# Two running sums per chunk for the convolution's taps, eight taps moved to GpSimd, two more gated pairs in three passes, the memory queries' copies ahead

## The chip, the cores and the metric

The kernel runs on one core of a Trainium2 chip. A core has five engines that each work through their own queue in order: TensorE (PE in the profile, with its weight loads as PEld), VectorE (DVE), ScalarE (ACT), GpSimd (POOL) and SyncE (SP), which here issues the loads of the weights. The metric is the device time of one execution in microseconds (us); lower is better. Before the change it is 976.33 us, the median of three runs (974.7 to 977.23).

## The reference

The kernel computes a decoder trunk of two layers on 256 tokens of width 1024 in fp32. Layer 0 is a SwiGLU feed-forward half step, then a mixer, then a second feed-forward half step; layer 1 has the same shape with another mixer. The change lies in the mixer of layer 0. Cut to that:

```python
u = hn @ a_w_in                                   # 1024 -> 768 + 768 + 256
a, gate = split(u[..., :1536], 2)                 # the gated pair
h = a * sigmoid(gate)
h = depthwise_conv(h, dw_kernel, 31 taps, causal) + dw_bias
primary = silu(layer_norm(h, ln_g, ln_b))         # mean and variance over the 768 channels
q_mem = u[..., 1536:]                             # 4 heads of 64, attention over 256 memory rows
mem_out = memory_attention(rms_norm(q_mem), ...)
h_out = x + concat(primary, mem_out) @ w_o
```

The convolution is per channel: for each of the 768 channels, 31 products of a shifted row of 256 tokens with one number are summed, and the bias is added.

## The kernel before

Activations lie transposed: 128 channels on the partitions, the 256 tokens along the free dimension. The 768 convolution channels are six chunks of 128 (c = 0 to 5). Weights come in chunks of 1 MB ([128, 2048], two halves of 1024 columns); one chunk holds the two halves of one gated pair, that is the 128 columns of `a` and of `gate` for one c. Three raw buffers hold loaded chunks.

**Three passes or whole.** TensorE multiplies either *in three passes* or *whole*. For three passes a half chunk is split by `half_chunk`: ACT makes the high part `wh` (`hi`, L184), DVE subtracts it from the raw weights to get the low part `wl` (`lo`, L188), and TensorE runs high x high, high x low and low x high (`mm3`); four `wh` and four `wl` buffers rotate. Whole, TensorE takes raw fp32 weights and activations (`whole_group`), and no other engine works on the weights. In `glu_in` the chunks c < `SPLIT_CHUNKS` (2) go in three passes and the others whole.

**Gating.** `glu_out` (high priority for the planner) scales the sums by the row norm (`cgs`, `cas` on DVE), takes the sigmoid on ACT (`cs`), and DVE writes the product into `hp` (L833; four smaller products, L838, for chunk 5). `hp` is the front of one large SBUF tile `hc`; the rest of `hc` holds `whole`, the convolution's results `cv` and the second layer's memory rows `my1`.

**Convolution.** `conv(c)` shares the 31 taps of a chunk between two engines, by `DVE_TAPS` = (14, 31, 0, 31, 18) and `POOL_TAPS` = (17, 0, 31, 0, 13) for chunks 0 to 4. DVE's share is one chain: the first tap writes a sum in PSUM (L857), each further tap is one `scalar_tensor_tensor` (L861), sum = window x tap + sum, reading the window in SBUF and the sum in PSUM. GpSimd's share: ACT writes the first tap with the bias into `cv` (L849), then for each further tap ACT scales the window into a buffer `cq` (L852; two buffers), and GpSimd adds it to `cv` (L853). Where both have a share, DVE adds its sum to `cv` at the end (L864). Chunk 5 is done on TensorE with diagonal matrices (`cvp`, L151). ACT also does eight scalings for `my1` (L876).

**What follows on TensorE**, in a fixed order: the memory queries' projection `mq`; the diagonal matmuls for chunk 5 (`cvp`); six steps of the second layer's memory keys and values (`mkv`); the transposes of the memory queries (`mq0p`, L154), which ACT copies out as `q0T` (L459, in `to_heads_T`); two more `mkv` steps; the scores of two pairs of memory heads (`am00s`, `am01s`), which need `q0T`; two `mkv` steps; and `lnm`, the mean over the channels, which takes the six chunks of `cv` in the order 5, 0, 1, 2, 3, 4. Between `mq` and `mq0p` lie ACT's squares (L434), DVE's sums and products (L436, L519, L521), GpSimd's power (L523) and DVE's last product (L526).

**Order.** From the convolution's start TensorE's instructions keep program order (`state["order"]`). The other engines' order is set by a planner when the kernel is built: it takes instructions as they get ready by its own estimate, those emitted earlier first, and those in `high_priority` before all. On the chip each queue then runs in that order. `behind(i, other)` makes instruction i come after `other` in the queue. Attention's steps later are in order by hand (`in_order`).

Of the kernel before, what the change touches and what calls it, by code (L numbers as in the profile page):

```python
# [9 lines left out]
F32 = mybir.dt.float32  # L10
# [3 lines left out]
AF = mybir.ActivationFunctionType  # L14
ALU = mybir.AluOpType
AX = mybir.AxisListType

P = 128
DM = 1024
KD = DM // P  # L20
SEQ = 256
NT = SEQ // P
DFF = 2816
KF = DFF // P
# [6 lines left out]
CC = PW // P  # L31
TAPS = 31
PAD = TAPS - 1
# [6 lines left out]
NB = 2 * MW  # L40
WARM = 12
MASKED = 1e30
SPLIT_CHUNKS = 2

DVE_TAPS = (14, 31, 0, 31, 18)
POOL_TAPS = (17, 0, 31, 0, 13)

HALF_CH = P // 2
SHIFTS = (TAPS + 1) // 2
# [1 line left out]
MEM_AT = 9  # L51
FIRST_CAT = 3
TURN_AT = 2
SLACK = 64
HOMES = {"ahs": 64, "bhs": 64, "chs": 64, "dhs": 64, "my0": 192, "by0": 192, "ay0": 128, "cat0": 128, "cat1": 128}
Q_AT = 6
# [29 lines left out]
def tile_kernel(ctx: ExitStack, tc: tile.TileContext, w, xT, memT, pos, vec, hg, const, out):  # L86
    nc = tc.nc
# [3 lines left out]
    tp = ctx.enter_context(tc.tile_pool(name="tp", bufs=2))  # L91
    op = ctx.enter_context(tc.tile_pool(name="op", bufs=4))
# [23 lines left out]
    q = HC // 2  # L116
# [14 lines left out]
    state = {"flip": False, "chunk": 0, "half": 0, "raw": None, "order": "", "last": {}}  # L131

    def behind(i, other):
        tc.add_manual_dep(i.ins, other.ins.name,
                          mybir.DependencyInfo(mybir.DependencyClass.NoSync, mybir.DependencyReason.DATA),
                          reason="issue order")
# [16 lines left out]
    def transp(*a, **k):  # L153
        in_order("P", nc.tensor.transpose(*a, **k))  # L154
# [44 lines left out]
    def tiles_of(n_half):  # L199
        for n in range(n_half):  # L200
            wh, wl = half_chunk()
            for i in range(8):
                yield wh[:, i * P:(i + 1) * P], wl[:, i * P:(i + 1) * P]
# [46 lines left out]
    def psum(name, tag="mm", bufs=4):  # L250
        return ps.tile([P, 512], F32, name=name, tag=tag, bufs=bufs)


    def at_home(t, name):
        a = HOMES.get(name, 0) // 4
        return t[:, a:a + t.shape[1] - SLACK].rearrange("p (k a s) -> p k a s", a=2, s=SEQ)

    def y_tiles(name):
        return at_home(yp.tile([P, KD * 2 * SEQ + SLACK], F32R, name=name, tag="y"), name)

    def y_both(name):
        whole = at_home(yp.tile([P, KD * 2 * SEQ + SLACK], F32, name=name + "w", tag="y"), name)
        return y_tiles(name), whole[:, :, 0]
# [67 lines left out]
    def ffn(name, y, acc, nexts, store=False, both=False, hook=None, after=None, hook_down=None, rb=None):  # L331

        hs = at_home(hp_.tile([P, KF * 2 * SEQ + SLACK], F32R, name=name + "hs", tag="hs"), name + "hs")
        first = acc is None
# [96 lines left out]
    def heads_norm(name, t, n):  # L431

        sq = tp.tile([P, MW], F32, name=name + "q", tag="sq")
        nc.scalar.activation(sq[:, :n * HD], t, AF.Square)  # L434
        ms = tp.tile([P, 4], F32, name=name + "m", tag="ms")
        nc.vector.tensor_reduce(ms[:, :n], sq[:, :n * HD].rearrange("p (h d) -> p h d", d=HD), axis=AX.X, op=ALU.add)  # L436
        return ms

    def rope(name, q3, t):

        n = q3.shape[1]
        a = tp.tile([P, 4, ROT], F32, name=name + "a", tag="ra")
        b = tp.tile([P, 4, ROT], F32, name=name + "b", tag="rbb")
        nc.vector.tensor_tensor(a[:, :n], q3[:, :, :ROT], cosT[:, t, None, :].to_broadcast([P, n, ROT]), op=ALU.mult)
        nc.vector.tensor_tensor(b[:, :n, :HALF], q3[:, :, HALF:ROT],
                                sinT[:, t, None, :HALF].to_broadcast([P, n, HALF]), op=ALU.mult)
        nc.vector.tensor_tensor(b[:, :n, HALF:], q3[:, :, :HALF],
                                sinT[:, t, None, HALF:].to_broadcast([P, n, HALF]), op=ALU.mult)
        nc.vector.tensor_tensor(q3[:, :, :ROT], a[:, :n], b[:, :n], op=ALU.add)

    def gain_b(g, n):
        return gt[:, None, g * HD:(g + 1) * HD].to_broadcast([P, n, HD])

    def to_heads_T(name, src, dst, pair0, t, tag="aux"):

        pp = psum(name, tag, 2)
        for i in range(2):
            transp(pp[:, i * P:(i + 1) * P], src[:, i * P:(i + 1) * P], ident)
        nc.scalar.activation(dst[:, pair0:pair0 + 2, t * P:(t + 1) * P],  # L459
                             pp[:, :2 * P].rearrange("p (a b) -> p a b", a=2), AF.Copy)  # L460

    def proj(name, y, *uses):

# [48 lines left out]
    def queries(name, e, g, dst, pair0, rot, scaler, defer=None):  # L512


        def use(t, o):
            ms = heads_norm(f"{name}s{t}", o, 4)
            qg = tp.tile([P, MW], F32, name=f"{name}t{t}", tag="tok")
            q3 = qg.rearrange("p (h d) -> p h d", d=HD)
            nc.vector.tensor_tensor(q3, o.rearrange("p (h d) -> p h d", d=HD), gain_b(g, 4), op=ALU.mult)  # L519
            v = tp.tile([P, 4], F32, name=f"{name}v{t}", tag="hv")  # L520
            nc.vector.tensor_scalar(v, ms, e[:, t:t + 1], None, op0=ALU.add)  # L521
            c = tp.tile([P, 4], F32, name=f"{name}c{t}", tag="hr")
            nc.gpsimd.tensor_tensor(c, v, mhalf[:, :4], op=ALU.pow)  # L523
            if rot:
                rope(f"{name}o{t}", q3, t)
            scaler.tensor_tensor(q3, q3, c[:, :, None].to_broadcast([P, 4, HD]), op=ALU.mult)  # L526
            def turn():
                to_heads_T(f"{name}p{t}", qg, dst, pair0, t, "aux" if defer is None else "sc")
            if defer is None:
                turn()  # L530
            else:
                defer.append(turn)
        return use
# [87 lines left out]
    def go(head, n):  # L621
        for _ in range(n):
            next(head)
# [148 lines left out]

    hc = hp_.tile([P, KF * 2 * SEQ + SLACK], F32, name="hc", tag="hs")
    hp = hc[:, :CC * (PAD + SEQ)].rearrange("p (c s) -> p c s", c=CC)
    whole = hc[:, CC * (PAD + SEQ):CC * (PAD + SEQ) + 2 * SEQ].rearrange("p (i s) -> p i s", i=2)
    cv = hc[:, KF * SEQ:KF * SEQ + CC * SEQ].rearrange("p (c s) -> p c s", c=CC)
    my1 = hc[:, (KF + CC) * SEQ:(KF + CC + KD) * SEQ].rearrange("p (k s) -> p k s", k=KD)
    nc.gpsimd.memset(hp[:, :, :PAD], 0.0)
    acc_p = [psum("cvp0", "aux", 2), psum("cvp1", "sc", 2)]

# [2 lines left out]
    tap = [[vt[:, V_TAP + c * TAPS + i:V_TAP + c * TAPS + i + 1] for i in range(TAPS)] for c in range(CC)]  # L783
    bias = [vt[:, V_CB + c:V_CB + c + 1] for c in range(CC)]
    rr = {}

    def whole_group(o, raw, i, ks):
        for k in ks:
            mmul(o[:, :SEQ], raw[:, (i * KD + k) * P:(i * KD + k + 1) * P], y[1][:, k], start=k == 0, stop=k == KD - 1)

    def glu_in(c):

        pa, pg = psum(f"ca{c}"), psum(f"cg{c}")
        if c == 0:
# [16 lines left out]
            return  # L811
        elif c < SPLIT_CHUNKS:
            for k, wt in enumerate(tiles_of(1)):
# [28 lines left out]
    def win(c, i):  # L842
        return hp[:, c, i:i + SEQ]

    def conv(c):
        nd, np_ = DVE_TAPS[c], POOL_TAPS[c]
        bi = bias[c]
        if np_:
            nc.scalar.activation(cv[:, c], win(c, nd), AF.Identity, scale=tap[c][nd], bias=bias[c])  # L849
            for i in range(nd + 1, nd + np_):  # L850
                q = tp.tile([P, SEQ], F32, name=f"cq{c}_{i}", tag="cvq")
                nc.scalar.activation(q, win(c, i), AF.Copy, scale=tap[c][i])  # L852
                state["pool"] = nc.gpsimd.tensor_tensor(cv[:, c], cv[:, c], q, op=ALU.add)  # L853
            bi = None
        if nd:
            o = acc_p[c == 1][:, (c == 3) * SEQ:((c == 3) + 1) * SEQ]
            nc.vector.tensor_scalar(o, win(c, 0), tap[c][0], bi, op0=ALU.mult,  # L857
                                    op1=ALU.bypass if bi is None else ALU.add)
            for i in range(1, nd):
                end = i == nd - 1 and bi is not None  # L860
                nc.vector.scalar_tensor_tensor(cv[:, c] if end else o, win(c, i), tap[c][i], o,  # L861
                                               op0=ALU.mult, op1=ALU.add)
            if bi is None:
                state["last"]["V"] = nc.vector.tensor_tensor(cv[:, c], o, cv[:, c], op=ALU.add)  # L864

    qT = cp.tile([P, 2, SEQ], F32, name="q0T", tag="q0T")
    kT, v = kv0
    for c in range(CC):
# [5 lines left out]
        if 0 < c < CC - 1:  # L874
            for k in range(2 * c - 2, 2 * c):
                behind(nc.scalar.activation(my1[:, k], mT[:, k], AF.Copy,  # L876
                                            scale=vt[:, V_MEM + KD + k:V_MEM + KD + k + 1]), state["func"])
# [5 lines left out]
    last = psum("cvp2")  # L883
# [3 lines left out]
    for g in range(2):  # L887
        for p in range(2):
            r = slice(p * HALF_CH, (p + 1) * HALF_CH)
            dst = cv[g * HALF_CH:(g + 1) * HALF_CH, CC - 1].rearrange("p (t q) -> p q t", q=2)[:, p]  # L890
# [17 lines left out]

    go(mem1, 6)
    for turn in turns:  # L910
        turn()
    go(mem1, 2)
    go(pairs[0], 1)
    go(pairs[1], 1)
# [87 lines left out]
    for k, (wh, wl, *_) in enumerate(halves):  # L1002
        for m in range(KD):
            s = slice(m * P, (m + 1) * P)
# [41 lines left out]
    n = len(pairs)  # L1046
    for p in range(n + 1):
        if p < n:
            go(pairs[p], 1)
        if p == TURN_AT:  # L1050
            for turn in turns:
# [142 lines left out]
```

## Time and profile before

| what | value |
|---|---|
| median of three runs | 976.33 us (974.7 to 977.23) |
| profiled execution, its own time | 976.35 us |
| its span, first to last instruction | 974.6 us |
| TensorE busy | 962.7 us, 99% of the span |
| VectorE busy | 743.9 us, 76% |
| ScalarE busy | 599.7 us, 62% |
| GpSimd busy | 123.6 us, 13% |
| granted TensorE clock | 1.00 |
| gated pairs, convolution, memory queries | about 204 to 270 us of the span |

Busy time is the sum of an engine's instructions. Rows of a timeline show the start, the length, the engine, the line, the operation and what it writes and reads; "xN" joins N neighbours of one kind. Instructions of DVE overlap a little at their edges, so that starts are nearer than lengths say. Rows of a line's own view show how many there are, the shortest, median and longest length in ns, and the first and last start.

### The profile page before, as it was taken

To read this page: it belongs to the slowest core of one execution; us is meant where nothing else is said; L and a number is where in the kernel's file an instruction comes from. 1 tells how busy PE (TensorE), PEld (TensorE's weight loads), DVE (VectorE), ACT (ScalarE), POOL (GpSimd) and SP (SyncE) were. 2 spreads that over 40 slices of the span, in tenths; PEclk is the share of its full clock that TensorE was granted. 3 is DMA by queue.
4 is the path that set the end of the run, shared out by engine and by line. 5 is a ranking of instruction groups with operands and counts; after the bars stand their busy time and mean duration, and the time that the engine had idled before them with its cause. 6 is when DMAs were issued, how large, how long until landed. Compare 5 with 4: busy or idle time off the path is not lost.

```text
span 974.6 us, 15375 instructions
## 1 busy us (share of the span) xinstructions
PE 962.7 (99%) x5784; PEld 840.1 (86%) x5784; DVE 743.9 (76%) x1328; ACT 599.7 (62%) x1154; POOL 123.6 (13%) x143
## 2 busy tenths in 40 slices
PE   8999999999999999999999999999998999999998
PEld 6888888898779888888888888888995898888887
DVE  7988776779977888777776877777789588888663
ACT  6676577857676665655556665565557656565542
POOL 0011000128713000000122000000152030000000
PEclk9999999999999999999999999999999999999999
DMA  8655555533325554555554555556442055555560
GB/s 312 241 199 179 197 189 188 202 130 131 114 102 188 204 213 174 203 186 176 203 183 174 183 206 178 207 177 212 177 174 87 27 194 213 180 210 174 190 219 23
DMA packets 26427, 173.47 MB, mean 178 GB/s; under 512 B 3184, under 2 KB 4848, under 8 KB 6000
## 3 DMA queue, kind: packets, MB, share of 16 engines
q1 hardware_dynamic: 26064, 172.31, 50.3%
q8 instruction: 45, 0.74, 0.3%
q14 instruction: 30, 0.25, 0.1%
q10 hardware_dynamic: 288, 0.17, 0.1%
HBM read 171.43 MB, written 1.05 MB: 177 GB/s over the span
## 4 chain that ended last, share of the span: by engine, by line
PE 92%; ACT 2%; DVE 2%; POOL 2%; DMA 1%; issue 1%; POOLq 0%; ACTq 0%; DVEq 0%
PE cg L151 7%; PE do L151 6%; PE bo L151 6%; PE dg L151 6%; PE bg L151 6%; PE bu L151 6%; PE co L151 6%; PE cu L151 6%; PE ao L151 6%; PE du L151 6%; PE ag L151 6%; PE au L151 6%; PE kv L151 3%; PE oao L151 2%; PE obo L151 2%; PE mkv L151 2%
## 5 line engine op out<-in xcount | busy, mean ns | idle before, releaser
L188 DVE TENSOR_TENSOR wl<-raw,wh 128x1024 fp32r<-128x1024 f32 (+1 forms) x310 | 377.0, 1220 | 94.6 <-ACT wh L184 89.6
L184 ACT ACTIVATE wh<-raw 128x1024 fp32r<-128x1024 f32 (+1 forms) x310 | 322.9, 1045 | 119.4 <-PE do L151 20.4
L151 PE MATMUL ag<-y,wh 128*128 128x512 f32 x176 | 46.9, 395 | 2.0 <-ACT wh L184 2.0
L151 PE MATMUL au<-y,wh 128*128 128x512 f32 x176 | 46.8, 393 | 0.0
L151 PE MATMUL bo<-bhs,wh 128*128 128x512 f32 (+1 forms) x198 | 45.4, 367 | 0.0
L151 PE MATMUL do<-dhs,wh 128*128 128x512 f32 (+1 forms) x198 | 45.4, 367 | 0.0
L151 PE MATMUL co<-chs,wh 128*128 128x512 f32 (+1 forms) x198 | 45.1, 366 | 0.0
L151 PE MATMUL ao<-ahs,wh 128*128 128x512 f32 (+1 forms) x198 | 45.0, 366 | 0.0
L151 PE MATMUL bg<-oay,wh 128*128 128x512 f32 x176 | 44.9, 393 | 0.0
L151 PE MATMUL cu<-by,wh 128*128 128x512 f32 x176 | 44.5, 393 | 0.0
L151 PE MATMUL dg<-oby,wh 128*128 128x512 f32 x176 | 44.5, 393 | 0.0
L151 PE MATMUL bu<-oay,wh 128*128 128x512 f32 x176 | 44.4, 392 | 0.0
L151 PE MATMUL du<-oby,wh 128*128 128x512 f32 x176 | 44.4, 392 | 0.0
L151 PE MATMUL cg<-by,wh 128*128 128x512 f32 x176 | 44.1, 392 | 0.0
L853 POOL TENSOR_TENSOR hc<-hc,cq 128x256 f32<-128x256 f32 x58 | 42.3, 730 | 12.9 <-ACT cq L852 9.1
L861 DVE SCALAR_TENSOR_TENSOR cvp<-hc,vt,cvp 128x256 f32<-128x256 f32 x88 | 40.6, 484 | 1.5
L151 PEld LDWEIGHTS ag<-y,wh 128*128 128x128 f32 x176 | 32.9, 188 | 9.4 <-ACT wh L184 2.5
L151 PEld LDWEIGHTS ao<-ahs,wh 128*128 128x128 f32 x198 | 34.7, 188 | 5.4
L151 PEld LDWEIGHTS do<-dhs,wh 128*128 128x128 f32 x198 | 34.7, 188 | 5.3
L151 PEld LDWEIGHTS bo<-bhs,wh 128*128 128x128 f32 x198 | 34.7, 188 | 5.3
L151 PEld LDWEIGHTS co<-chs,wh 128*128 128x128 f32 x198 | 34.6, 188 | 5.4
L151 PEld LDWEIGHTS cg<-by,wh 128*128 128x128 f32 x176 | 33.0, 188 | 7.1
(996 smaller groups left out, 2118.5 us busy)
## 6 DMA issues: line engine op xcount, KB each, us to landing
raw<-in_w SPq DMA_DIRECT2D x158, 1024.0 KB, 4.8
raw<-in_w SPq DMA_DIRECT2D x5, 512.0 KB, 9.2
mT<-in_memT SPq DMA_DIRECT2D x1, 1024.0 KB, 8.7
out<-x SPq DMA_DIRECT2D x8, 128.0 KB, 1.7
raw<-in_w SPq DMA_DIRECT2D x2, 256.0 KB, 4.0
x<-in_xT SPq DMA_DIRECT2D x1, 512.0 KB, 7.5
x<-in_xT SPq DMA_DIRECT2D x2, 128.0 KB, 3.6
x<-in_xT SPq DMA_DIRECT2D x1, 256.0 KB, 5.0
```

Of the source, the lines that this page charges most:

```text
L151: return in_order("P", nc.tensor.matmul(*a, **k))
L184: state["act"] = nc.scalar.activation(wh[:, s], raw[:, s], AF.Copy)
L188: state["dve"] = nc.vector.tensor_tensor(wl[:, s], raw[:, s], wh[:, s].bitcast(F32), op=ALU.subtract)
L853: state["pool"] = nc.gpsimd.tensor_tensor(cv[:, c], cv[:, c], q, op=ALU.add)
L861: nc.vector.scalar_tensor_tensor(cv[:, c] if end else o, win(c, i), tap[c][i], o, op0=ALU.mult, op1=ALU.add)
```

## The change

`SPLIT_CHUNKS` goes from 2 to 4: the pairs of chunks 2 and 3 are computed in three passes, with `wh` and `wl` made by ACT and DVE. Each engine's share of a chunk's taps is added up in two sums in turn, even taps into one and odd taps into the other. On DVE the first sum stays in PSUM; the second is `spare[:, 1]`, a part of `hc`, for chunks 0 and 4, and `cv[:, c]`, also in `hc`, for chunks 1 and 3. One add joins the two, and for chunks 0 and 4 a second add joins GpSimd's part. On GpSimd the sums are `cv[:, c]` and `spare[:, 0]`, ACT writes the first two taps, and one more add joins them. The `cq` buffers become four places in `spare`. Eight of chunk 4's taps go from DVE to GpSimd. Last, the fourth scaled tap from the end is put behind the two copies `q0T` on ACT.

```diff
-SPLIT_CHUNKS = 2
-
-DVE_TAPS = (14, 31, 0, 31, 18)
-POOL_TAPS = (17, 0, 31, 0, 13)
+SPLIT_CHUNKS = 4
+
+DVE_TAPS = (14, 31, 0, 31, 10)
+POOL_TAPS = (17, 0, 31, 0, 21)
+CQ_BUFS = 4
...
+BEHIND = 4
...
-        nc.scalar.activation(dst[:, pair0:pair0 + 2, t * P:(t + 1) * P],
-                             pp[:, :2 * P].rearrange("p (a b) -> p a b", a=2), AF.Copy)
+        return nc.scalar.activation(dst[:, pair0:pair0 + 2, t * P:(t + 1) * P],
+                                    pp[:, :2 * P].rearrange("p (a b) -> p a b", a=2), AF.Copy)
...
+    spare = hc[:, 10 * SEQ:(12 + CQ_BUFS) * SEQ].rearrange("p (k s) -> p k s", s=SEQ)
...
         if np_:
-            nc.scalar.activation(cv[:, c], win(c, nd), AF.Identity, scale=tap[c][nd], bias=bias[c])
-            for i in range(nd + 1, nd + np_):
-                q = tp.tile([P, SEQ], F32, name=f"cq{c}_{i}", tag="cvq")
-                nc.scalar.activation(q, win(c, i), AF.Copy, scale=tap[c][i])
-                state["pool"] = nc.gpsimd.tensor_tensor(cv[:, c], cv[:, c], q, op=ALU.add)
+            sums = cv[:, c], spare[:, 0]
+            for n, i in enumerate(range(nd, nd + np_)):
+                if n < 2:
+                    nc.scalar.activation(sums[n], win(c, i), AF.Identity, scale=tap[c][i],
+                                         bias=bias[c] if n == 0 else 0.0)
+                    continue
+                q = spare[:, 2 + len(scaled) % CQ_BUFS]
+                scaled.append(nc.scalar.activation(q, win(c, i), AF.Copy, scale=tap[c][i]))
+                nc.gpsimd.tensor_tensor(sums[n % 2], sums[n % 2], q, op=ALU.add)
+            nc.gpsimd.tensor_tensor(cv[:, c], *sums, op=ALU.add)
             bi = None
         if nd:
             o = acc_p[c == 1][:, (c == 3) * SEQ:((c == 3) + 1) * SEQ]
-            nc.vector.tensor_scalar(o, win(c, 0), tap[c][0], bi, op0=ALU.mult,
-                                    op1=ALU.bypass if bi is None else ALU.add)
-            for i in range(1, nd):
-                end = i == nd - 1 and bi is not None
-                nc.vector.scalar_tensor_tensor(cv[:, c] if end else o, win(c, i), tap[c][i], o,
+            sums = o, spare[:, 1] if np_ else cv[:, c]
+            for i in range(nd):
+                if i < 2:
+                    b = bi if i == 0 else None
+                    nc.vector.tensor_scalar(sums[i], win(c, i), tap[c][i], b, op0=ALU.mult,
+                                            op1=ALU.bypass if b is None else ALU.add)
+                    continue
+                nc.vector.scalar_tensor_tensor(sums[i % 2], win(c, i), tap[c][i], sums[i % 2],
                                                op0=ALU.mult, op1=ALU.add)
-            if bi is None:
-                state["last"]["V"] = nc.vector.tensor_tensor(cv[:, c], o, cv[:, c], op=ALU.add)
+            last = nc.vector.tensor_tensor(sums[1], *sums, op=ALU.add)
+            if np_:
+                last = nc.vector.tensor_tensor(cv[:, c], sums[1], cv[:, c], op=ALU.add)
+            state["last"]["V"] = last
...
     for turn in turns:
-        turn()
+        behind(scaled[-BEHIND], turn())
```

More of the change, by code (lines that the diff above doesn't have):

```diff
@@ L527, in turn @@
             def turn():
-                to_heads_T(f"{name}p{t}", qg, dst, pair0, t, "aux" if defer is None else "sc")
+                return to_heads_T(f"{name}p{t}", qg, dst, pair0, t, "aux" if defer is None else "sc")
             if defer is None:
@@ L777, in tile_kernel @@
     my1 = hc[:, (KF + CC) * SEQ:(KF + CC + KD) * SEQ].rearrange("p (k s) -> p k s", k=KD)
+    spare = hc[:, 10 * SEQ:(12 + CQ_BUFS) * SEQ].rearrange("p (k s) -> p k s", s=SEQ)
+    assert 10 * SEQ >= CC * (PAD + SEQ) + 2 * SEQ and 12 + CQ_BUFS <= KF
     nc.gpsimd.memset(hp[:, :, :PAD], 0.0)
@@ L785, in tile_kernel @@
     rr = {}
+    scaled = []
     def whole_group(o, raw, i, ks):
```

## The prediction

> **What bounds the kernel now.** I read the page first, then the chain of waits between 204 and 310 us, then the timelines of VectorE (DVE), GpSimd (POOL) and ScalarE (ACT) there.
>
> ```profile
> PE 962.7 (99%) x5784; PEld 840.1 (86%) x5784; DVE 743.9 (76%) x1328; ACT 599.7 (62%) x1154; POOL 123.6 (13%) x143
> PE 92%; ACT 2%; DVE 2%; POOL 2%; DMA 1%; issue 1%; POOLq 0%; ACTq 0%; DVEq 0%
> 210.30:243.30 33.00, 33.00 (x178) 29.69 (x177) 31.85 (x76) 23.52 (x52) 24.99 (x35) 1.00 0.28 101
> 243.30:268.50 25.20, 23.93 (x134) 18.52 (x133) 22.76 (x52) 15.47 (x34) 19.39 (x26) 1.00 0.34 120
> ```
>
> TensorE sets the time of the whole; its clock is 1.00. The windows' columns are PE, weight loads, DVE, ACT, POOL. The change touches only this stretch, the convolution's, where DVE is busy 31.85 of 33.00 us beside a busy TensorE: a second engine with no room. In the second window TensorE lacks 1.27 us, and the chain shows why:
>
> ```profile
> 265.06 0.51 ACT cq L852
> 265.60 0.39 ACT q0T L459
> 266.03 1.19 PE am00s L151 x6
> 270.21 2.59 PE lnm L151 x12
> PE am00s L151 <- ACT q0T L459: 1.3, 1, 1.3
> ```
>
> The copies q0T stand on ACT behind scaled taps that wait for GpSimd. TensorE then runs to lnm, the mean over the six chunks, which ends at 272.80 and takes chunk 4 last.
>
> **What the change gains if nothing collides.** Pairs three and four go from whole fp32 to three passes:
>
> ```profile
> 210.32 2.74 PE ca L151 x24
> 213.06 2.73 PE cg L151 x24
> 215.78 3.45 PE ca L151 x16
> 219.24 3.47 PE cg L151 x16
> ```
>
> Chunk 1 is a pair in three passes, 5.47; chunk 2 a whole one, 6.92. Two pairs save 2 x 1.45 = **2.90 us** of TensorE. The copies ahead can take away the 1.27. Together -4.17.
>
> For it DVE gets four subtractions and ACT four conversions. The taps change pitch:
>
> ```profile
> 205.26 1.22 DVE L188 TENSOR_TENSOR wl<-raw,wh 128x1024 fp32r<-128x1024 f32 x1
> 219.85 2.82 DVE L861 SCALAR_TENSOR_TENSOR cvp<-hc,vt,cvp 128x256 f32<-128x256 f32 x7
> 246.51 4.69 DVE L861 SCALAR_TENSOR_TENSOR cvp<-hc,vt,cvp 128x256 f32<-128x256 f32 x9
> 259.10 8.89 DVE L861 SCALAR_TENSOR_TENSOR cvp<-hc,vt,cvp 128x256 f32<-128x256 f32 x17
> ```
>
> Where two chunks' taps alternate a tap starts (2.82-0.48)/6 = 0.39 us after the one before; in a single chain (8.89-0.49)/16 = 0.525. Two sums turn the second into the first, 0.135 each. Up to 257.7 us some 27 steps run at the long pitch (8 of them in the row at 246.51): -3.5. The subtractions add 4 x 1.22 = 4.9, two more merges about 0.7. So up to there DVE has +2.1 us more; only after it do the eight taps less and the last chain's 16 steps give back. [...]
>
> ACT's new work (4 x 1.06, 8 scaled taps at 0.40 from start to start, two bias-form starts) is about 8 us and lies in ACT's free 9.5 and 9.7 us of the two windows; without that cover it would cost up to its 8. The weights' raw chunks come free at the subtraction instead of after the matmuls, and DMA is busy 0.28 of the window: the loads stay hidden.
>
> **What collides.** The second sum lies in SBUF (`spare`, or `cv`), where the first lies in PSUM. So taps 3, 5, 7... read two SBUF operands: 6 + 14 + 14 + 4 = 38 of the 78 chained taps, besides the subtractions and the final adds. Before, no chained tap did. What such a product costs beside GpSimd's adds stands in the trace:
>
> ```profile
> 211.78 0.43 DVE L833 TENSOR_TENSOR hc<-cas,cs 128x256 f32<-128x256 f32 x1 [0.21 <-ACT cs L829]
> 217.07 0.51 DVE L833 TENSOR_TENSOR hc<-cas,cs 128x256 f32<-128x256 f32 x1
> 218.03 6.38 POOL L853 TENSOR_TENSOR hc<-hc,cq 128x256 f32<-128x256 f32 x8 [0.73 <-ACT cq L852]
> 223.98 0.71 DVE L833 TENSOR_TENSOR hc<-cas,cs 128x256 f32<-128x256 f32 x1
> 230.91 0.75 DVE L833 TENSOR_TENSOR hc<-cas,cs 128x256 f32<-128x256 f32 x1
> 231.95 7.24 POOL L853 TENSOR_TENSOR hc<-hc,cq 128x256 f32<-128x256 f32 x9 [0.57 <-ACT cq L852]
> 238.56 0.91 DVE L833 TENSOR_TENSOR hc<-cas,cs 128x256 f32<-128x256 f32 x1
> L526 DVE TENSOR_TENSOR mq0t<-mq0t,mq0c x2: 729/839/949, 256.1 to 257.7; 128x256 f32<-128x256 f32 x2
> L282 DVE SCALAR_TENSOR_TENSOR my<-mT,vt,my x8: 474/479/481, 51.2 to 54.4; 128x256 fp32r<-128x256 f32 x8
> L282 DVE SCALAR_TENSOR_TENSOR cy<-x,vt,cy x8: 483/966/974, 662.4 to 712.0; 128x256 fp32r<-128x256 f32 x8
> 311.44 0.80 POOL L291 TENSOR_TENSOR oaacc<-oaacc,oaq 128x256 f32<-128x256 f32 x1
> 311.56 0.96 DVE L282 SCALAR_TENSOR_TENSOR oay<-x,vt,oay 128x256 fp32r<-128x256 f32 x1
> 312.31 0.81 POOL L291 TENSOR_TENSOR oaacc<-oaacc,oaq 128x256 f32<-128x256 f32 x1
> ```
>
> Alone the product takes 0.43. With GpSimd at work it ends 0.28 us after GpSimd's add ends: 224.41 and 224.69, then 239.19 and 239.47. L282 is the very form of a tap on the second sum (two SBUF operands, one scalar): 0.48 alone, 0.97 beside adds; and an add beside it ends 0.60 after it (312.52, 313.12), so that adds go 0.875 apart. One SBUF operand is enough to stay clear: the taps keep 0.48 while GpSimd is busy throughout (the row of x7). The Trainium skill has this in "SBUF — State Buffer", "Who interferes with whom": a DVE instruction with two SBUF inputs contends with a GpSimd one that reads SBUF, and the later one blocks fully. By that rule, an add would follow in full, 0.73 after the tap and not 0.60; the trace agrees but for this 0.13.
>
> GpSimd's adds themselves:
>
> ```profile
> L853 POOL TENSOR_TENSOR hc<-hc,cq x58: 722/728/792, 213.3 to 265.9; 128x256 f32<-128x256 f32 x58
> 226.60 0.73 POOL L853 TENSOR_TENSOR hc<-hc,cq 128x256 f32<-128x256 f32 x1
> 227.29 0.73 POOL L853 TENSOR_TENSOR hc<-hc,cq 128x256 f32<-128x256 f32 x1
> POOL hc L853 <- ACT cq L852: 9.1, 8, 4.1
> ```
>
> Two adds on different sums start 0.69 apart, on one sum (7.24-0.73)/8 = 0.81. GpSimd goes from 58 to 66. Its sum: 66 x 0.69 = 45.5; 45 meetings with two-operand work (38 taps, a final add, four L833, two L526) x (0.875-0.69) = 8.3; two subtractions of pair four in the way, about 1.0 each, 2.0; the two powers of the memory queries as before, 2.2; waits for ACT, 5.0 before without the first and 1 to 5 now with four buffers, taken as 2.5. That is 60.5 us from about 214.0 (pair three's subtractions push the first gated product back by some 0.7), so to **274.5**, against 266.64 before: the eight taps moved go to the engine that the second sum slows.
>
> DVE is an in-order queue, so its waits add up ahead of all that stands behind. How long one wait is depends on where in an add it falls. If first-sum and second-sum taps alternate strictly, two taps fit in an add's 0.875 where they took 0.78: 0.095 for each second-sum tap. At the other end is L282's 0.49. The means over an unblocked one are 0.29 (L833: 0.08, 0.29, 0.32, 0.48), 0.41 (L526) and 0.49 (L282, cy): I take their middle, **0.40**, for taps of two chunks will interleave and adds start unaligned to them.
>
> What TensorE waits for in DVE's queue:
>
> ```profile
> 245.15 1.33 DVE L838 TENSOR_TENSOR hc<-cas,cs 64x128 f32<-64x128 f32 x4
> 250.15 5.07 PE L151 MATMUL cvp<-hc,diag 128*128 128x128 f32 x44
> 257.71 0.95 DVE L526 TENSOR_TENSOR mq0t<-mq0t,mq0c 128x256 f32<-128x256 f32 x1
> 262.45 0.60 PE L154 MATMUL mq0p<-cst,mq0t 128*128 128x128 f32 x4
> ```
>
> Chunk 5's gated rows end at 246.48 and cvp needs them at 250.15, after the change at 247.25. Ahead of them stand 30 new two-operand instructions (6 + 14 + 7 taps, a final add, two subtractions): 12.0 us. With 2.90 earlier input and 2.1 more work they come at 257.7; TensorE stands 10 us, and all that follows it in program order with it. The queries' second product ended at 258.66 with 3.8 us to spare before mq0p. Seven more taps stand ahead of it: 258.66 - 2.90 + 2.1 + 37 x 0.40 = 272.7. So mq0p goes from 262.45 to 272.7, +10.25. From there to am00s there was the 1.27, which the copies ahead do save: **+9.0 us** at am00s, and at lnm. Chunk 4 isn't later: its last four scaled taps now stand on ACT behind the copies, which wait for mq0p (done by 274.0), and GpSimd waits for them; the four adds, the merge and the final add end near 278.8, where lnm wants it about 281. Nothing after 310 us has room to give the time back, TensorE being full. The profiled execution took 976.35 us, its span 974.6 and 1.75 around it; that is the median shown (976.33). 976.35 + 9.0 = **985.3**.
>
> **Rivals.** *No collision* (the taps slip between adds, as the one at 217.07 nearly did, 0.08): -4.17, 972.2. For it only that one; against it the L282 rows beside an add. *Strict alternation*: 0.095 each, 3.5 us for the 37, mq0p's cover holds all but that; then GpSimd's end decides. 274.5, final add 0.43, lnm's last step 0.45: 275.4 against 272.80, +2.6, 978.9. For it, emission in turns; against it, two chunks' taps side by side, as in the row of x7. *The subtractions of pair four come too late*: they carry no priority and are emitted behind chunk 1's taps, whose last ended at 242.5 (first row below). From pair four's start (219.24 + 3.47 = 222.7) to mq0p lay 39.8 us, now 38.3; TensorE, at pair four by 221.1, would wait until 242.5 and come to mq0p at 280.8: +18.3 - 1.27 = +17.1, 993.4. It decides once DVE's queue has the taps first. Against it: later-emitted work does get between taps,
>
> ```profile
> 242.07 0.47 DVE L861 SCALAR_TENSOR_TENSOR hc<-hc,vt,cvp 128x256 f32<-128x256 f32 x1
> 253.16 0.42 DVE L519 TENSOR_TENSOR mq0t<-mq,gt 128x256 f32<-128x256 f32 x1
> ```
>
> as the queries' product (second row) does between two taps of chunk 3.
>
> **How the numbers follow.** Chances: no collision 0.13, strict alternation 0.20, the forecast 0.58, late subtractions 0.09. The forecast's own range, waits of 0.25 to 0.49: +3.4 to +12.3, 980 to 989. The range of all, 975 to 991, leaves out the first and most of the last. About 0.3% (2.9 us) is what a measurement can tell from no change. Faster: 0.13; half of strict alternation falls within: 0.11; slower: 0.76.
>
> **What would show it.** Second-sum taps with a median well over 0.48 and first-sum taps at 0.48; adds near 0.80 rather than 0.73, ending after 274; TensorE standing ahead of cvp and of mq0p; the pairs at 5.47. Wrong would be: second-sum taps at 0.48, or no idle ahead of cvp.

## The result, and the profile after

| | kernel before | kernel after |
|---|---|---|
| median, same chip | 976.18 us (974.7 to 977.23) | 983.98 us (983.49 to 986.48) |
| ratio, 95% interval | | 1.0087 (1.0075 to 1.0099) |
| profiled execution, its span | 974.6 us | 982.2 us |

The change makes the kernel 0.87% slower, 7.8 us. The forecast was 985.3 with a range of 975 to 991. The groups of the profile after that answer to those shown of before, from the views of two lines (count, then shortest, median and longest ns, first and last start) and the page's groups:

```profile
L874 DVE SCALAR_TENSOR_TENSOR cvp<-hc,vt,cvp x40: 472/476/490, 216.6 to 274.4; 128x256 f32<-128x256 f32 x40
L874 DVE SCALAR_TENSOR_TENSOR hc<-hc,vt x38: 469/556/1001, 217.0 to 270.8; 128x256 f32<-128x256 f32 x38
L862 POOL TENSOR_TENSOR hc<-hc 128x256 f32<-128x256 f32 x63 | 52.1, 858 | 10.0 <-ACT hc L861 9.9
```

First-sum taps take 0.476 us, where a chained tap took 0.48 before; the 38 second-sum taps reach from 0.469 to 1.001. The mean length of GpSimd's adds went from 0.73 to 0.858.

TensorE's timeline after, cut to the rows that the prediction named:

```profile
241.90 7.07 PE L153 MATMUL mq<-raw,ay0w 128*128 128x256 f32 x32
254.74 9.33 PE L153 MATMUL cvp<-hc,diag 128*128 128x128 f32 x64 [5.77 <-DVE hc L843]
...
269.06 0.38 PE L156 MATMUL mq0p<-cst,mq0t 128*128 128x128 f32 x2
269.68 0.44 PE L156 MATMUL mq0p<-cst,mq0t 128*128 128x128 f32 x2 [0.24 <-DVE mq0t L528]
272.95 1.58 PE L153 MATMUL am00s<-mk,q0T 64*128 64x256 f32 x7 [1.11 <-ACT q0T L461]
277.37 2.75 PE L153 MATMUL lnm<-hc,onem 128*128 128x256 f32 x12
```

The same places before, two of which the prediction hadn't shown, and the chain's rows where chunk 0's pair starts, before and then after:

```profile
243.25 1.03 PE L151 MATMUL mq<-raw,ay0w 128*128 128x256 f32 x4
270.05 2.75 PE L151 MATMUL lnm<-hc,onem 128*128 128x256 f32 x12
204.04 2.48 PE ca L151 x21
```

```profile
203.45 2.47 PE ca L153 x21
```

The stage starts 0.59 earlier on the span after, so 0.59 is added to each difference. The delay grows from -0.76 at `mq` (241.90 - 243.25 + 0.59) to +5.18 at `cvp`, +7.20 at `mq0p`, +7.51 at `am00s` and +7.91 at `lnm`. The spans differ by 7.6, with the same 0.59 added by 8.2: nothing behind `lnm` makes or gives back much.

So TensorE stands 5.77 ahead of `cvp`, where the prediction put its first wait. But ahead of `mq0p` it hardly waits, because `cvp` itself took 9.33 in place of 7.31. The view by windows (length; PE, weight loads, DVE, ACT, POOL busy; granted clock; DMA share and GB/s) shows the clock:

```profile
249.00:254.70 5.70, 0.00 (x0) 0.00 (x0) 5.67 (x12) 3.63 (x8) 3.73 (x6) 0.76 0.55 184
254.70:260.00 5.30, 5.26 (x30) 5.27 (x30) 5.21 (x9) 3.83 (x9) 5.30 (x8) 0.61 0.00 0
252.00:258.50 6.50, 3.76 (x17) 3.77 (x18) 6.38 (x12) 5.62 (x14) 5.04 (x7) 0.50 0.16 67
```

DVE is busy in nearly all of it. From 254.70 to 260.00 the matmuls run at a mean clock of 0.61, and within that the clock stands at half, 0.50, until 258.50 and beyond (last row); the prediction had nothing of the kind.

The groups of DVE's lines between 204 and 270 us show work that the prediction left out as well. After, then before:

```profile
L838 DVE TENSOR_TENSOR hc<-cas,cs 128x256 f32<-128x256 f32 x7 | 5.4, 778 | 0.0
L836 DVE TENSOR_TENSOR cas<-ca,cnb 128x256 f32<-128x256 f32 x8 | 3.3, 412 | 0.0
```

```profile
L833 DVE TENSOR_TENSOR hc<-cas,cs 128x256 f32<-128x256 f32 x5 | 3.3, 661 | 0.2 <-ACT cs L829 0.2
L831 DVE TENSOR_TENSOR cas<-ca,cnb 128x256 f32<-128x256 f32 x6 | 2.5, 415 | 0.0
```

Six chunks are gated, but the product stands seven times in place of five (chunk 5's are another line), the scaling `cas` eight times in place of six, and `cgs` likewise. The reason is a line that the diff doesn't touch. In `glu_in` chunk 0 is gated from within the loop over the pairs in three passes:

```python
        elif c < SPLIT_CHUNKS:
            for k, wt in enumerate(tiles_of(1)):
                mm3(pa[:, :SEQ], wt, y[0], k, k == 0, k == KD - 1)
                if k == 0:
                    glu_out(0, *rr["p"])
```

With `SPLIT_CHUNKS` at 2 that is once. At 4 it is three times, for c = 1, 2 and 3, and writes the same rows again: 2 x (0.778 + 2 x 0.412) = 3.2 us of DVE by these lengths, less at the edges.

### The profile page after: what moved, and what is told of

Same layout as the page of the kernel before. It is cut to its first block, busy times and chain, and to the rows that moved or that the text cites. A ratio compares the mean times of both kernels' runs of the same rounds, so it can differ in the third digit from the quotient of the medians.

```text
span 982.2 us, 15477 instructions
## 1 busy us (share of the span) xinstructions
PE 963.9 (98%) x5816; PEld 841.6 (86%) x5816; DVE 754.6 (77%) x1334; ACT 606.3 (62%) x1168; POOL 135.3 (14%) x151
## 4 chain that ended last, share of the span: by engine, by line
PE 90%; DVE 4%; ACT 2%; issue 1%; DMA 1%; POOL 1%; POOLq 0%; DVEq 0%; ACTq 0%
PE cg L153 6%; PE do L153 6%; PE bo L153 6%; PE dg L153 6%; PE bg L153 6%; PE bu L153 6%; PE co L153 6%; PE cu L153 6%; PE ao L153 6%; PE du L153 6%; PE ag L153 6%; PE au L153 6%; PE kv L153 3%; PE oao L153 2%; PE obo L153 2%; PE mkv L153 2%
## 5 line engine op out<-in xcount | busy, mean ns | idle before, releaser
L190 DVE TENSOR_TENSOR wl<-raw,wh 128x1024 fp32r<-128x1024 f32 (+1 forms) x314 | 382.0, 1220 | 95.3 <-ACT wh L186 90.4
L186 ACT ACTIVATE wh<-raw 128x1024 fp32r<-128x1024 f32 (+1 forms) x314 | 327.0, 1045 | 123.9 <-PE do L153 20.1
L862 POOL TENSOR_TENSOR hc<-hc 128x256 f32<-128x256 f32 x63 | 52.1, 858 | 10.0 <-ACT hc L861 9.9
L153 PEld LDWEIGHTS bu<-oay,wh 128*128 128x128 f32 x176 | 32.9, 188 | 7.0
```

The source lines that it names most:

```text
L153: return in_order("P", nc.tensor.matmul(*a, **k))
L186: state["act"] = nc.scalar.activation(wh[:, s], raw[:, s], AF.Copy)
L190: state["dve"] = nc.vector.tensor_tensor(wl[:, s], raw[:, s], wh[:, s].bitcast(F32), op=ALU.subtract)
L862: nc.gpsimd.tensor_tensor(sums[n % 2], sums[n % 2], q, op=ALU.add)
```

## The experiments

Theory, from the prediction: the second sum lies in SBUF, so its taps and GpSimd's adds wait for one another. Main rival: the added load (subtractions, joins, two sums as such) is what costs. Each ratio is against the kernel before, timed beside it on the same chip; kernels timed at different hours are compared by their ratios.

### The second sum, put elsewhere or done alone

The first four runs take the change apart. In PSUM (`e1`), chunks 0, 1 and 3:

```diff
+            acc_q = [psum("cvr0", "aux", 2), psum("cvr1", "sc", 2)]
-            sums = o, spare[:, 1] if np_ else cv[:, c]
+            joined = spare[:, 1] if np_ else cv[:, c]
+            sums = o, joined if c == CC - 2 else acc_q[c == 1][:, :SEQ]
```

> The changed kernel with DVE's second sum in PSUM (two more banks) for chunks 0, 1 and 3; only chunk 4's four odd taps and the joining adds still read two SBUF operands. Nothing is left out. Theory 'collision' (a tap that reads two SBUF operands waits for GpSimd's add, and the add for it): the odd taps go back from a mean of 0.66 us to 0.48, GpSimd's adds from 0.86 to about 0.74, TensorE doesn't stand ahead of cvp (5.8 us in the changed kernel), the time falls by 8 to 12 us to 972 to 976. Rival 'load' (DVE, ACT and GpSimd simply have too much work with the two pairs' subtractions and conversions, the added adds and the eight taps): same instructions, so the same 982 to 986.

Measured: 979.17, ratio 1.0018 (1.0009 to 1.0028). Most of the loss is gone, but less than the collision theory gave. The same kernel once more:

> The kernel with the second sums of chunks 0, 1 and 3 in two further PSUM banks once more (979.17 measured), for a profile of it. With the sums of all chunks in one further bank 975.96 was measured. If chunk 4's four SBUF taps are the difference of 3.2, they stand at 0.8 to 0.95 in the profile and TensorE waits about 3 us at chunk 4's end or ahead of the memory scores. If the second further bank is, TensorE waits 2 to 4 us for a bank, ahead of work that needs one, with the taps at 0.48.

Measured: 977.31, ratio 1.0013 (1.0001 to 1.0025). Its taps by the view of their line:

```profile
L875 DVE SCALAR_TENSOR_TENSOR cvr<-hc,vt,cvr x31: 472/477/483, 217.5 to 263.6; 128x256 f32<-128x256 f32 x31
L875 DVE SCALAR_TENSOR_TENSOR hc<-hc,vt x4: 473/754/840, 244.2 to 254.0; 128x256 f32<-128x256 f32 x4
```

In PSUM a second-sum tap takes 0.477; only chunk 4's four in SBUF take 0.754. TensorE still waits 1.40 ahead of `cvp`, 1.2 in the fourth pair and 0.76 for `q0T`. Neither answer that was expected fits by itself: the four taps are slow, but their excess is about 1 us, and the one wait that may be for a bank, the 1.2 in the fourth pair, is under the 2 to 4 us and stands in the kernel with one further bank too (`e6`, below).

DVE with one sum, as before (`e2`), all else as after:

```diff
-            sums = o, spare[:, 1] if np_ else cv[:, c]
...
-            last = nc.vector.tensor_tensor(sums[1], *sums, op=ALU.add)
+            for i in range(1, nd):
+                end = i == nd - 1 and bi is not None
+                nc.vector.scalar_tensor_tensor(cv[:, c] if end else o, win(c, i), tap[c][i], o,
```

> The changed kernel with one sum per chunk on DVE, in PSUM, as in the kernel before; GpSimd keeps its two sums, the eight taps and the pairs in three passes stay. Nothing is left out. Theory 'collision': no tap waits for an add; DVE has 4 x 1.22 us of subtractions more and 8 taps less (8 x 0.53 = 4.2) than before, so about the load of before, and TensorE 2.9 less: 973 to 978. Rival 'load': two sums were the saving (0.135 us at each of some 40 steps, 5 us), without them DVE is later still: 986 to 991.

Measured: 973.46, ratio 0.9962 (0.995 to 0.9974), faster than both kernels. With the same pairs, the same repeated gating and the same taps on GpSimd, TensorE has hardly a wait left (DVE's timeline with a run of taps, then TensorE's):

```profile
246.25 4.80 DVE L871 SCALAR_TENSOR_TENSOR cvp<-hc,vt,cvp 128x256 f32<-128x256 f32 x12
```

```profile
247.50 7.31 PE L153 MATMUL cvp<-hc,diag 128*128 128x128 f32 x64
```

The load alone is not what costs: that rival expected 986 to 991. And the twelve taps start (4.80 - 0.48)/11 = 0.39 apart with a single sum for each chunk, since the planner lets two chunks alternate. The faster pitch that the second sum was to bring is there without it.

The other way round, before with DVE's two sums alone (`e3`; the `conv` of after for DVE, everything else as before):

> The kernel before with one part of the change alone: DVE adds its taps into two sums, the second in SBUF; taps, pairs, GpSimd's single sum and ACT's order are those of before. Nothing is left out. Theory 'collision': 42 odd taps read two SBUF operands and wait 0.19 us on average as in the changed kernel (0.66 less 0.48), 8 us, against 5 us won at the long steps; GpSimd's adds rise from 0.73 to 0.85 and end 5 us later or more, about 272 instead of 266.6 us: 978 to 984. Rival 'load': DVE saves 5 us and nothing else changes: 974 to 976.

Its second-sum taps by the view of their line, and TensorE's timeline:

```profile
L865 DVE SCALAR_TENSOR_TENSOR hc<-hc,vt x42: 467/556/1028, 214.6 to 263.7; 128x256 f32<-128x256 f32 x42
```

```profile
256.05 9.89 PE L151 MATMUL cvp<-hc,diag 128*128 128x128 f32 x64 [4.75 <-DVE hc L839]
```

Measured: 985.16, ratio 1.0075 (1.0054 to 1.0096), a little above what was expected. This one part has the taps, the idle ahead of `cvp` and the slow `cvp` of the whole change, and nearly its loss.

### GpSimd's adds taken away

The kernel after without the line `nc.gpsimd.tensor_tensor(sums[n % 2], sums[n % 2], q, op=ALU.add)` (`e5`):

> The kernel after, with GpSimd's adds of the scaled taps left out (its part of chunks 0, 2 and 4 is therefore missing from the sums; ScalarE's scalings, the joining adds and everything of VectorE are kept). Collision theory: the second-sum taps in SBUF are slow only beside GpSimd's adds, so their median falls from 0.556 to 0.48 and the mean from 0.663 to 0.48-0.50; TensorE no longer stands 5.8 us ahead of the diagonal matmuls, its clock there stays at 1.00, and the time is 970 to 974. Rival, the place itself: a tap that reads and writes SBUF on both sides costs 0.19 more whatever GpSimd does, the median stays near 0.556, the idle stays above 3 us and the time is 979 to 984.

The same two views:

```profile
L873 DVE SCALAR_TENSOR_TENSOR hc<-hc,vt x38: 471/478/630, 216.4 to 257.3; 128x256 f32<-128x256 f32 x38
```

```profile
247.30 7.31 PE L153 MATMUL cvp<-hc,diag 128*128 128x128 f32 x64
```

Measured: 973.84, ratio 0.998 (0.9971 to 0.9989). The same taps at the same place take 0.478 once GpSimd is still. That is the collision theory's answer. The time alone would not decide it, since ScalarE no longer waits for GpSimd here either; the length of the taps does.

### All second sums in PSUM

Chunks 0 and 4 in the free half of the second sum's bank, 1 and 3 in one further bank (`e6`):

```diff
+            odd = acc_p[1] if c != 1 and c != 3 else acc_q
+            sums = o, odd[:, (c != 1) * SEQ:((c != 1) + 1) * SEQ]
```

> The kernel after, with the second sums of all four chunks in PSUM: chunks 0 and 4 in the free half of the second sum bank, chunks 1 and 3 in one further bank; only the last tap of each second sum writes SBUF. If the 979.17 with two further banks came from chunk 4's four SBUF taps or from a bank that was missed elsewhere, this one comes to 971 to 975 by the collision theory. Rival, the two sums themselves: a chain that runs at 0.39 per tap in place of 0.525 takes VectorE away from other work at another time, so that some wait stays wherever the sum lies: 977 to 981, with second-sum taps at 0.48.

Measured: 975.96, ratio 0.9996 (0.9986 to 1.0007), between the two answers' main values. Against the kernel after that is about 0.9% less: the place in SBUF alone is worth all of the loss. (The Trainium skill, "SBUF — State Buffer", section "Who interferes with whom": a DVE instruction with at most one SBUF input, outside the two-port modes, does not contend with GpSimd. The 31 taps at 0.477 above agree.) Against `e2` two sums still cost some 0.3%. TensorE's two waits in its timeline:

```profile
220.62 0.47 PE L153 MATMUL ca<-ay,wh 128*128 128x256 f32 x2 [1.20 <-ACT hc L861]
262.94 1.19 PE L153 MATMUL am00s<-mk,q0T 64*128 64x256 f32 x7 [1.25 <-ACT q0T L461]
```

Together 2.45 us. The first names ACT, but DVE's scaling `cas` (220.06, 0.41 long) ends 0.15 ahead of the matmul, as it does at the kernel after's wait in this place (222.20 and 222.35), so it is more likely that scaling. The second is for the copies on ACT, in whose queue the work stands in another order than in `e2`; why the planner chose it stays open.

### The change's other parts

Before with `SPLIT_CHUNKS` at 4 and nothing else (`e4`):

> The kernel before with one part of the change alone: the third and fourth gated pairs in three passes. Nothing is left out. Theory 'collision': TensorE has 2.9 us less, DVE 4.9 us more, so that the convolution's end on DVE (268.5 us, lnm wants it by 272) becomes what lnm waits for: 268.5 + 4.9 = 273.4 against 272 less 2.9, a net of 0 to +3: 975 to 980; the taps keep 0.48. Rival 'load': the conversions and subtractions are the main cause of the changed kernel's loss: 981 to 986.

Measured: 980.09, ratio 1.0024 (1.0011 to 1.0038), at the edge of what the collision theory gave. Then the kernel of `e2` with chunk 4's taps back at 18 and 13 (`e8`), with no copies ahead (`e7`: `turn()` without `behind`), and with one sum on GpSimd too (`e10`).

> The kernel after with one PSUM sum per chunk on VectorE (973.46 measured), and chunk 4's taps back at 18 for VectorE and 13 for GpSimd. Eight taps at 0.525 on VectorE put the end of chunk 4 from 267.7 to about 271.9 on the span, where the mean over the channels took its last step at about 268.5: a wait of 2 to 4 us and 975.5 to 978 if moving the taps was worth it by itself. Rival: chunk 4 is hidden either way, 973 to 974.

> The kernel after with one sum per chunk on VectorE (in PSUM, 973.46 measured) and also one on GpSimd. GpSimd's adds on one sum start 0.81 apart where two sums gave 0.69: 63 x 0.12 less three joining adds of 0.73 is 5.4 us more, so GpSimd ends at about 272 in place of 266.75, the mean over the channels waits 3 to 5 us for chunk 4, and the time is 976.5 to 979. Rival, GpSimd's pitch is hidden: 973 to 974.

> The kernel after with one PSUM sum per chunk on VectorE (973.46 measured) and without the order that puts the queries' copies ahead of the last four scaled taps. If that order is worth what the wait of before was (1.27), 974.3 to 975.5 with a wait of about 1 us ahead of the memory scores. If the four buffers alone or GpSimd's two sums did it, 973.0 to 974.0 and no such wait.

Measured: 978.33, ratio 1.0024 (1.0014 to 1.0033), for `e8`; 976.65, ratio 1.0014 (1.0003 to 1.0026), for `e10`; 972.07, ratio 0.9966 (0.9956 to 0.9976), for `e7`. `e8` is just above the range of its first answer, `e10` inside. TensorE's rows at `lnm` and behind it, of `e4`, of `e8`, of `e10` (whose profiled execution took 979.91, the longest of its ten) and last of `e2`:

```profile
272.02 0.70 PE L151 MATMUL lnm<-hc,onem 128*128 128x256 f32 x2 [2.03 <-DVE hc L864]
272.55 5.29 PE L151 MATMUL mkv<-raw,hc 128*128 128x512 f32 x8
```

```profile
271.16 1.03 PE L153 MATMUL lnm<-hc,onem 128*128 128x256 f32 x2 [3.38 <-DVE hc L874]
271.98 5.01 PE L153 MATMUL mkv<-raw,hc 128*128 128x512 f32 x8
```

```profile
271.22 1.22 PE L153 MATMUL lnm<-hc,onem 128*128 128x256 f32 x2 [3.22 <-DVE hc L871]
272.23 5.96 PE L153 MATMUL mkv<-raw,hc 128*128 128x512 f32 x8
```

```profile
266.19 2.75 PE L153 MATMUL lnm<-hc,onem 128*128 128x256 f32 x12
268.77 3.60 PE L153 MATMUL mkv<-raw,hc 128*128 128x512 f32 x8
```

In all three `lnm` waits for chunk 4, 2.0 to 3.4 us, and the eight matmuls behind take 1.4 to 2.4 longer than in `e2`. So the pairs pay only when chunk 4 ends in time, and that takes the eight moved taps and GpSimd's two sums together. The copies ahead are worth nothing that can be told here: with and without them the ratios' intervals overlap, and `e7` has no wait of 1 us ahead of `am00s`. Of the two answers the second holds: without that order there is no such wait either.

### Does the idle bring the clock down?

Matmuls that nothing uses, in the place where TensorE stood idle (`e11`, and `e12` with 13 in place of 26):

```diff
     last = psum("cvp2")
+    for k in range(26):
+        mmul(last[:, :SEQ], onem, y[1][:, k % KD], start=True, stop=True)
```

> The kernel after with 26 more fp32 matmuls of 128x256 ahead of the diagonal matmuls, about 5.6 us, into the bank that these overwrite; they stand where TensorE stood idle 5.8 us, and nothing uses their result. If the granted clock of 0.61 behind the idle comes from the idle, the clock stays at 1.00, the 64 diagonal matmuls take 7.31 in place of 9.33, and the time falls by about 2 from 983.98 to 981 to 983 though TensorE has 5.6 us more to do. Rival, the clock falls there for another reason: they stay at 9 or more, and the time is 983.5 to 985.5.

Each matmul turned out to be two instructions, and the filling 11.39 us long: 987.0, ratio 1.0116 (1.0099 to 1.0133). The right length:

> The kernel after with 13 more matmuls (26 instructions of 0.216, 5.6 us) ahead of the diagonal matmuls, where TensorE stood idle 5.8 us; the bank is overwritten, nothing uses the result. With 26 of them (52 instructions, 11.39 us, measured) the diagonal matmuls went 5.2 us too late, but at 7.31 in place of 9.33. If it is the idle that brings the clock down, here they start at about 254.7 as in the kernel after, take 7.3 and the time is 981 to 983. Rival, the diagonal matmuls were short there only because they were late: 9 or more again, and 983.5 to 985.5.

Measured: 987.4, ratio 1.011 (1.0089 to 1.0131). TensorE's timeline in it:

```profile
247.99 5.78 PE L153 MATMUL cvp<-ay0w,onem 128*128 128x256 f32 x26
254.11 7.41 PE L153 MATMUL cvp<-hc,diag 128*128 128x128 f32 x64 [0.34 <-DVE hc L843]
269.04 0.44 PE L156 MATMUL mq0p<-cst,mq0t 128*128 128x128 f32 x2 [1.69 <-DVE mq0t L528]
274.40 2.35 PE L153 MATMUL am00s<-mk,q0T 64*128 64x256 f32 x8 [3.20 <-ACT q0T L461]
```

`cvp` takes 7.41 in place of 9.33: it is the idle that brings the clock down. But the 2 us weren't saved. `mq0p` now waits 1.69 for the queries' second product, and its second part starts 14.93 behind `cvp`'s start (269.04 - 254.11), where in the kernel after it is 14.94 (269.68 - 254.74). There the slow clock had filled that very wait. (At `am00s` this kernel loses more, as ACT's copies of chunk 5 came ahead of `q0T` in its queue.) That the time would fall by 2 was wrong.

## Why the prediction was right, and where not

**Pairs, -2.90.** Nearly reached, and only without the collision: in `e2` `mq` starts 2.4 earlier than before (240.60 on its span, its stage starting 0.27 earlier than before's). After, 0.76 was left, since TensorE waited in the fourth pair:

```profile
222.35 0.47 PE L153 MATMUL ca<-ay,wh 128*128 128x256 f32 x2 [1.73 <-DVE cas L836]
```

That chunk 0's banks, held for its third gating, leave two banks for the rest would explain why a pair waits for a scaling at all; it is argued, and no run here gates chunk 0 once.

**DVE's load, +2.1.** Wrong in two places. The repeated gating, up to 3.2, was missing. And the pitch gain was booked on the second sum, though alternating chunks have it without: from one start to the next in DVE's timeline, up to the queries' second product, a chained tap takes 0.430 on average before and 0.399 in `e2`, and a first-sum tap 0.394 after. Over the 73 taps of before that is 2.6 us, where 3.5 had been worked out.

**The wait of a second-sum tap, 0.40.** The collision is what the prediction said (`e5`), but the size is wrong: the page's view by groups has, up to 270 us,

```profile
L874 DVE SCALAR_TENSOR_TENSOR hc<-hc,vt 128x256 f32<-128x256 f32 x37 | 24.4, 666 | 0.0
L874 DVE SCALAR_TENSOR_TENSOR cvp<-hc,vt,cvp 128x256 f32<-128x256 f32 x34 | 16.2, 476 | 0.0
```

so 0.666 - 0.476 = **0.19** each, under the range's 0.25. The timelines of GpSimd and DVE show why:

```profile
241.64 0.72 POOL L862 TENSOR_TENSOR hc<-hc 128x256 f32<-128x256 f32 x1 [0.44 <-ACT hc L861]
241.79 0.85 DVE L874 SCALAR_TENSOR_TENSOR hc<-hc,vt 128x256 f32<-128x256 f32 x1
269.94 0.56 DVE L874 SCALAR_TENSOR_TENSOR hc<-hc,vt 128x256 f32<-128x256 f32 x1
```

Of the 38 second-sum taps 32 end 0.28 or 0.29 after an add of GpSimd ends (here 241.64 + 0.72 + 0.28 = 241.79 + 0.85), the same 0.28 that the prediction found at the gated products; the other six took 0.47. So the wait depends on where in an add a tap falls. At 269.94, one sum after the other in step with the adds, a tap takes 0.56: the strict alternation, 0.08 (0.095 had been worked out). At 241.79 DVE alternates the sums too, but GpSimd had just waited 0.44 for ScalarE, so that its add began shortly before the tap, which then took 0.85. Both of the cases that the prediction held apart occur, and the value to take was between the two, not the middle of the blocked rows.

**Chunk 5's rows.** They ended at 256.16 (the first row below), where 257.7 was worked out; TensorE stood 5.77, not 10.

```profile
255.43 0.73 DVE L843 TENSOR_TENSOR hc<-cas,cs 64x128 f32<-64x128 f32 x1
268.68 0.94 DVE L528 TENSOR_TENSOR mq0t<-mq0t,mq0c 128x256 f32<-128x256 f32 x1
```

**The queries' second product.** At 269.62 (the second row), with the 0.59 at 270.2, so 2.5 before the 272.7: 37 waits shorter by 0.21 are 7.8 less; the forgotten gating is up to 3.2 more, chunk 5's four products, at 0.608 each where they took 0.319, 1.2 more, and the smaller pitch gain 0.9 more. That is roughly the whole. That `mq0p` waits for it holds, though the profile after shows only 0.24: in `e12`, with the clock up, the wait stands there in full, and `mq0p` is no earlier.

**The copies ahead, -1.27.** They didn't save it. ACT's timeline after:

```profile
271.99 0.51 ACT L861 ACTIVATE hc<-hc,vt 128x256 f32<-128x256 f32 x1 [1.23 <-POOL hc L862]
272.52 0.38 ACT L461 ACTIVATE q0T<-mq0p 128x256 f32<-128x256 f32 x1
272.80 0.50 ACT L861 ACTIVATE hc<-hc,vt 128x256 f32<-128x256 f32 x1
273.20 0.37 ACT L461 ACTIVATE q0T<-mq0p 128x256 f32<-128x256 f32 x1
273.46 0.51 ACT L861 ACTIVATE hc<-hc,vt 128x256 f32<-128x256 f32 x1
```

The first copy stands on ACT right behind a scaled tap that had waited for an add of GpSimd, and `am00s` waits 1.11, where before it was 1.27. The prediction took the last four scaled taps to stand behind the copies. The edit binds only one, the fourth from the end (`scaled[-BEHIND]`), and one scaled tap is all that stands behind the second copy.

**GpSimd's end, 274.5.** It was 276.41 (the row below): GpSimd began its adds at 215.06 rather than about 214.0 and took 61.4 rather than 60.5. From one start to the next, where it did not stand idle, its adds came 0.82 apart on average, and the sum had (45.5 + 8.3)/66 = 0.815. Its waits for ACT are 9.9, of which 6.4 lie ahead of the first add. `lnm` wanted chunk 4 at about 280 and did not wait for it: this step held.

```profile
275.69 0.72 POOL L863 TENSOR_TENSOR hc<-hc 128x256 f32<-128x256 f32 x1
```

**The sum.** +9.0 was worked out, +7.5 measured at `am00s`. That it is near is luck: with the wait as measured, 37 x 0.19 = 7.0, the prediction's own sum gives 258.66 - 2.90 + 2.1 + 7.0 = 264.9 for `mq0p` and +1.1 at `am00s`. Errors of both signs met: waits half as long, against the gating, chunk 5's products, the pitch and the wait for `q0T`. The mechanism, its place and its order (first `cvp`, then `mq0p`) are shown; the closeness of the number isn't evidence for its terms. *No collision* at 972.2 is what `e2` and `e5` do when the collision is taken away: 973.46 and 973.84.

## What to carry to other kernels

Before giving a VectorE chain a second sum, see whether the chain's pitch is short already through other work between its links, and keep the operands that it reads beside a busy GpSimd down to one in SBUF. When a constant grows that bounds a loop, count every call in the loop, also those that the diff doesn't show, and check the instruction counts by line against the number of tiles. Before filling an idle stretch of an engine, ask which wait comes next behind it.

## What was not expected of the hardware

TensorE's granted clock can drop after an idle stretch, and the drop outlasts it. The window of `e4` behind its wait of 2.03:

```profile
272.00:278.00 6.00, 5.98 (x13) 2.87 (x14) 5.89 (x17) 5.41 (x22) 0.00 (x0) 0.72 0.00 0
```

In the kernel after the low clock reads 0.50, half of full (the row from 252.00 to 258.50 above). By that, 0.72 over 6.00 us is half speed for (1 - 0.72) x 6.00 / 0.5 = 3.4 us. The kernel after has, over its two windows, (0.24 x 5.70 + 0.39 x 5.30) / 0.5 = 6.9 us, twice as much. So an idle stretch of 2 us cost its own length and 1.7 more (the eight `mkv` matmuls at 5.29, in `e2` at 3.60).

No shortest idle stretch that brings the drop can be read from these runs. The waits of 1.40 in `e9` and 1.69 in `e12` left the next matmuls at full speed. But in the second layer TensorE waits for the same thing in every kernel, and the same wait did both, in `e9` (first row) and in `e12`:

```profile
739.68 1.08 PE L156 MATMUL am10pp<-cst,am10p 128*128 128x128 f32 x4 [1.44 <-ACT am11p L572]
749.36 0.63 PE L156 MATMUL am10pp<-cst,am10p 128*128 128x128 f32 x4 [1.44 <-ACT am11p L572]
```

In `e9` the clock read 0.50 from 740 to 743 us, in `e12` 1.00 throughout. The profiled executions of the kernel after, `e2` and `e7` have such a drop there and that of before has none, so a difference of 0.1 or 0.2% between two kernels may be one drop more or less.

The Trainium skill has this in "TensorE: Matmul & The Clock Gate", section "What's actually happening": a monitor halves the clock after an idle window of about 3.4 us and gives it back after a busy one. The drops of 3.4 and 6.9 us agree with windows of that length; that the idle must last about a window doesn't, as 2.03 us were enough in `e4` and 1.44 in `e9`.
